# Query projection with channels on the partitions, its norm put in with the logits, in the second layer of a hybrid decoder

## The chip, the cores and the metric

The kernel is one program on one core of one Trainium2 chip. The metric is device microseconds (us) of one launch. The engines are named as the profile names them: PE is TensorE (PEld its weight loads), DVE is VectorE, ACT is ScalarE, POOL is GpSimd and SP is SyncE, which issues transfers.

## The reference, cut to what matters

Two layers over 1024 tokens of width 1024. The first is a gated DeltaNet, which the change leaves alone. The second is attention in a window of 128 keys, with 32 query heads of 64 channels that share 4 key and value heads, a norm over each query head, a bias by distance and a sink:

```
q, z = jnp.split(h @ w_in, 2, axis=-1)
q = rms_norm(q.reshape(B, T, B_Q_HEADS, B_HD), q_gain) * (B_HD ** -0.5)
logits = jnp.einsum("bnqkgd,bnskd->bnkgqs", q, k_band) + bias     # then the mask
m = jnp.maximum(jnp.max(logits, axis=-1, keepdims=True), sink)
p = jnp.exp(logits - m)
probs = p / (jnp.sum(p, axis=-1, keepdims=True) + jnp.exp(sink - m))
o = jnp.einsum("bnkgqs,bnskd->bnqkgd", probs, v_band)
return (o.reshape(B, T, B_W) * jax.nn.silu(z)) @ w_out
```

The norm of a query is one number per token and head, so it may be applied to q, or to the logits before the bias is added.

## The kernel before, in words

All large products are made in three matmuls of 32-bit operands that are split in a high and a low part: high by high, high by low, low by high. The transposed input `hT` lies in SBUF in that split form, with tokens as columns.

The second layer works in 8 groups of 4 query heads (256 channels). For each group `b_q` projects the queries, `b_z` (twice) projects the gate, and `b_attend` goes through 8 blocks of 128 tokens. Each of `b_q` and `b_z` takes its weights from a queue: a transfer of 512 KB that SP issues into `wraw` (two buffers), a multiplication by the input norm's gain on POOL (two halves, L153), a cast to the high part on ACT (L155) and a subtraction for the low part on DVE (L157). Four sets of split weights are held, so a weight can be cast only when PE has finished with the one four places earlier.

PE's order is that of the program; the other engines' orders come from a scheduler. `interleave` weaves the two strands together: `b_attend` yields amounts of time, and that much projection is put in at each yield. One block of attention goes to PE in four visits with projection between them: `turn` (four transposes of the probabilities of block i, L1197), `q_turn` (two transposes of the normalised queries of block i+3, L1149), `logits` (twelve matmuls for block i+2, L1174) and `values` (up to eight matmuls for block i-1, L1218). Around these matmuls a block needs on DVE two predicated copies (L1178) and four additions of the bias with a minimum (L1182), on ACT four exponentials (L1187), on DVE a reciprocal (L1189), and on POOL the multiplication of the probabilities by it (L1191).

Before the change `gemm_tc` (L983 to L985) projects the queries with tokens on the partitions: the stationary operand is 128 tokens of `hT`, and 256 channels are streamed. A group takes 8 x 8 x 3 = 192 such matmuls. The result is copied to SBUF (L1107), squared (L1109), summed per head (L1110), and multiplied by the inverse root (L1115); then `q_turn` transposes it for the logits. The gate already uses `gemm_ct` (L180 to L184), in which the stationary operand is 128 channels of the weight and 512 tokens are streamed.

A number of small jobs (`later`) are put off by a number of ticks; a tick is one step of contraction in `gemm_ct`, and two such steps in `gemm_tc`.

Of the kernel before, what the change touches and what calls it, by code (L numbers as in the profile page):

```python
# [18 lines left out]
P = 128  # L19
# [45 lines left out]
class Kernel:  # L65
# [122 lines left out]
    def consts(self, ctx):  # L188
# [10 lines left out]
        self.identr = cp.tile([P, P], F32R, name="identr")  # L199
        nc.vector.tensor_copy(self.identr, self.ident)  # L200
# [835 lines left out]
    class Group:  # L1036


        def __init__(self, hg):
            self.hg, self.q, self.ot, self.zs, self.left = hg, [], [], [], 5  # L1040

    def layer_b(self, last):
# [7 lines left out]
        for _ in steps:  # L1050
            for _ in range(4):
                next(first)
        for _ in first:
            pass
        self.flush()
# [5 lines left out]
        raws = lambda j: bp.tile([P, 2, 512], F32, name="qr", bufs=3)  # L1061
# [30 lines left out]
    def b_q(self, X):  # L1092

        nc, bp, sb = self.nc, self.bp, self.sb
        ws = [self.take(), self.take()]
        for half in range(2):
            qr = bp.tile([P, 4, 256], F32, name="qr", bufs=3)
            ss = sb.tile([P, 4, 4], F32, name="ssqb")
            for c in range(4):
                n = half * 4 + c  # L1100
                if c % 2 == 0:
                    ps = self.mm.tile([P, 2, 256], F32, name="mm")
                yield from self.gemm_tc(ps[:, c % 2, :], ws, n)
# [34 lines left out]
    def b_attend(self, groups):  # L1138
# [3 lines left out]
        qT, Ls, pTs = {}, {}, {}  # L1142

        def q_turn(i):
# [254 lines left out]
```

## Time and profile before

| | us |
|---|---|
| median of 3 runs | 1867.74 (1866.12 to 1868.64) |
| the profiled execution, its own time | 1867.72 |
| span of its trace | 1866.0 |
| PE busy | 1809.7 (97% of the span) |
| DVE busy | 1231.2 (66%) |
| ACT busy | 730.7 (39%) |
| POOL busy | 514.0 (28%) |

The span is from the first to the last instruction; 1.7 us of the execution's time lie outside it. Matmuls overlap in time and their ends are modelled, so the busy time of PE says only that it does not stand still; what one matmul costs is read from the distance between the starts of two neighbours. In the trace the second layer's first query projection starts at about 1130 us, its attention runs from 1155 to about 1690 us, and the output projection ends the program.

### The profile page before, as it was taken

The page shows a single profiled execution, that of the slowest core. Times are in us where ns is not written, and L with a number is a line of the kernel's source. Part 1 is how long each engine was busy: PE and PEld are TensorE (multiplying, and loading weights), DVE is VectorE, ACT ScalarE, POOL GpSimd, SP SyncE. Part 2 cuts the span into 40 slices and gives each one's busy share as a digit, 9 for nine tenths or more (in the row PEclk, how much of TensorE's full clock was granted, in tenths as well). Part 3 has the DMA queues.
Part 4 walks back from the last instruction along what each step waited for, and adds up shares of the span by engine and source line. Part 5 has one row for each costly group of instructions (what it writes and reads, how often), then busy time and mean ns, then how long its engine had stood idle before and what let it go on. Part 6 is the DMA issues. An engine that isn't in the chain of part 4 may idle for free.

```text
span 1866.0 us, 31106 instructions
## 1 busy us (share of the span) xinstructions
PE 1809.7 (97%) x11778; PEld 1466.0 (79%) x11778; DVE 1231.2 (66%) x2895; ACT 730.7 (39%) x1813; POOL 514.0 (28%) x629
## 2 busy tenths in 40 slices
PE   6999999999999998999999999999999999999999
PEld 6667778787878776778788899887787787777887
DVE  6777776868586778765545365777776766763432
ACT  6446362634445364523112042444444444441100
POOL 1323232323222233221311231333333323221211
PEclk9999999999999999999999999999999999999999
DMA  4611111112011111122655331111111111225552
GB/s 151 134 49 35 57 46 46 47 35 69 23 58 35 58 34 47 45 91 92 236 170 171 122 92 46 30 46 46 63 41 52 57 34 59 68 69 201 182 169 102
DMA packets 134874, 149.55 MB, mean 80 GB/s; under 512 B 7242, under 2 KB 91716, under 8 KB 134724
## 3 DMA queue, kind: packets, MB, share of 16 engines
q1 hardware_dynamic: 124384, 130.40, 22.5%
q10 hardware_dynamic: 10340, 17.16, 2.9%
q8 instruction: 93, 1.52, 0.3%
q14 instruction: 57, 0.47, 0.1%
HBM read 116.05 MB, written 31.49 MB: 79 GB/s over the span
## 4 chain that ended last, share of the span: by engine, by line
PE 77%; DVE 10%; issue 3%; POOL 3%; ACT 1%; DMA 1%; POOLq 0%; DVEq 0%; ACTq 0%; SPq 0%
PE mm L180 9%; PE mm L182 9%; PE mm L184 9%; PE acc L933 6%; PE acc L932 6%; PE acc L931 6%; PE mm L983 4%; PE mm L984 4%; PE mm L985 4%; PE pv L1218 3%; PE lg L1174 3%; DVE acc L494 2%; PE tp L1197 1%; DVE wlo L157 1%; PE kqp L693 1%
## 5 line engine op out<-in xcount | busy, mean ns | idle before, releaser
L180 PE MATMUL mm<-hh,whi 128*128 128x512 f32 (+1 forms) x1040 | 428.0, 412 | 2.5 <-ACT hh L246 2.4
L182 PE MATMUL mm<-hl,whi 128*128 128x512 f32 (+1 forms) x1040 | 417.9, 402 | 1.5 <-DVE hl L247 1.5
L184 PE MATMUL mm<-hh,wlo 128*128 128x512 f32 (+1 forms) x1040 | 415.4, 399 | 0.0
L157 DVE TENSOR_TENSOR wlo<-wraw,whi 128x512 fp32r<-128x512 f32 x292 | 205.8, 728 | 225.0 <-POOL whi L150 192.4
L150 POOL TENSOR_SCALAR whi<-wraw 128x1024 fp32r<-128x1024 f32 x110 | 121.3, 1103 | 474.7 <-PE acc L933 240.7
L180 PEld LDWEIGHTS mm<-hh,whi 128*128 128x128 f32 x1040 | 197.0, 189 | 39.1 <-issue 4.6
L184 PEld LDWEIGHTS mm<-hh,wlo 128*128 128x128 f32 x1040 | 196.9, 189 | 37.3 <-issue 4.2
L182 PEld LDWEIGHTS mm<-hl,whi 128*128 128x128 f32 x1040 | 197.2, 190 | 35.6 <-issue 4.2
L983 PE MATMUL mm<-whi,hh 128*128 128x256 f32 x608 | 183.6, 302 | 0.0
L984 PE MATMUL mm<-wlo,hh 128*128 128x256 f32 x608 | 171.9, 283 | 0.0
L985 PE MATMUL mm<-whi,hl 128*128 128x256 f32 x608 | 171.8, 283 | 0.0
L494 DVE SCALAR_TENSOR_TENSOR acc<-u,cw,acc 128x512 f32<-128x512 f32 x192 | 152.9, 798 | 22.0 <-POOL acc L491 19.6
L1187 ACT ACTIVATE lsb<-lsb,m 128x129 f32<-128x129 f32 x256 | 100.4, 394 | 165.2 <-DVE m L1182 129.3
L983 PEld LDWEIGHTS mm<-whi,hh 128*128 128x128 f32 x608 | 115.8, 190 | 14.7 <-issue 10.0
L1191 POOL TENSOR_TENSOR lsb<-lsb,den 128x512 f32<-128x512 f32 x64 | 72.9, 1139 | 189.2 <-DVE den L1189 177.6
L153 POOL TENSOR_TENSOR wraw<-wraw,gcolb 128x512 f32<-128x512 f32 x72 | 79.0, 1117 | 140.4 <-DMA wraw<-in_b_w_in 96.7
L984 PEld LDWEIGHTS mm<-wlo,hh 128*128 128x128 f32 x608 | 116.1, 191 | 0.2
L985 PEld LDWEIGHTS mm<-whi,hl 128*128 128x128 f32 x608 | 115.8, 190 | 0.0
L491 POOL TENSOR_SCALAR acc<-u,cw 128x512 f32<-128x512 f32 x64 | 57.0, 891 | 183.4 <-ACT u L487 169.9
L931 PE MATMUL acc<-whi,hh 128*128 128x512 f32 x256 | 99.7, 389 | 0.0
L933 PE MATMUL acc<-whi,hl 128*128 128x512 f32 x256 | 99.6, 389 | 0.0
L932 PE MATMUL acc<-wlo,hh 128*128 128x512 f32 x256 | 99.6, 389 | 0.0
(352 smaller groups left out, 3722.0 us busy)
## 6 DMA issues: line engine op xcount, KB each, us to landing
wraw<-in_a_w_in SPq DMA_DIRECT2D x48, 512.0 KB, 4.0
wraw<-in_a_w_out SPq DMA_DIRECT2D x32, 512.0 KB, 3.6
wraw<-in_b_w_in SPq DMA_DIRECT2D x32, 512.0 KB, 4.0
wraw<-in_b_w_out SPq DMA_DIRECT2D x32, 512.0 KB, 3.9
og<-zs SPq DMA_DIRECT2D x32, 256.0 KB, 2.0
ogT<-zs SPq DMA_DIRECT2D x24, 256.0 KB, 2.1
btab<-lt SPq DMA_DIRECT2D x1, 4096.0 KB, 24.3
dm<-gd SPq DMA_DIRECT2D x8, 512.0 KB, 4.1
```

What stands on the lines that cost most here:

```text
L150: nc.gpsimd.tensor_scalar(out=hi, in0=raw, scalar1=1.0, scalar2=1.0, op0=ALU.mult, op1=ALU.mult)
L157: nc.vector.tensor_tensor(out=lo[:, ks], in0=raw[:, ks], in1=self.f32(hi[:, ks]), op=ALU.subtract)
L180: nc.tensor.matmul(ps, hi[:, k, :], hh[:, k, :], start=(k == 0), stop=False)
L182: nc.tensor.matmul(ps, hi[:, k, :], hl[:, k, :], start=False, stop=False)
L184: nc.tensor.matmul(ps, lo[:, k, :], hh[:, k, :], start=False, stop=(k == KT - 1))
L494: nc.vector.scalar_tensor_tensor(out=acc, in0=u[:, t:t + 512], scalar=cw[:, t, blk:blk + 1], in1=acc, op0=ALU.mult, op1=ALU.add)
L931: nc.tensor.matmul(ps[c], oh[:, k, ts], hi[:, kk, :], start=(k4 + k == 0), stop=False)
L932: nc.tensor.matmul(ps[c], oh[:, k, ts], lo[:, kk, :], start=False, stop=False)
L933: nc.tensor.matmul(ps[c], ol[:, k, ts], hi[:, kk, :], start=False, stop=(k4 + k == 6))
L983: nc.tensor.matmul(ps, hh[:, k, ts], hi[:, k % 4, :], start=(k == 0), stop=False)
L984: nc.tensor.matmul(ps, hh[:, k, ts], lo[:, k % 4, :], start=False, stop=False)
L985: nc.tensor.matmul(ps, hl[:, k, ts], hi[:, k % 4, :], start=False, stop=(k == KT - 1))
```

## The change

The queries are now projected by `gemm_ct`: a group takes 2 halves x 2 pairs of heads x 24 = 96 matmuls with 512 columns, and the result already has the channels on the partitions, as the logits want it. It is split in high and low (`qr`, `ql`) at once, without the norm. `q_turn` is gone. The squares are transposed in 32 x 32 pieces and summed on DVE (`part`), and 16 ticks later `b_sums` adds up the pieces with one matmul against a constant and makes the inverse root of the mean square, and the root itself, in small steps on DVE. The norm goes in at the logits: a new step `rows` on POOL divides the bias by it ahead of time, and the DVE instruction that adds the bias takes the norm as its scale. `values` is emitted directly behind `logits`. The queries' weights come in the form that the gate's have. The order of projections changes by one place: the third query projection now comes ahead of the first gate projection. An unused tile is dropped.

```diff
     def b_order():
-        order = [("q", 0, 0), ("q", 1, 0), z.pop(0)]
+        order = [("q", 0, 0), ("q", 1, 0)]
         for hg in range(2, 8):
             order += [("q", hg, 0), z.pop(0), z.pop(0)]
...
     def b_q(self, X):
         ws = [self.take(), self.take()]
         for half in range(2):
-            qr = bp.tile([P, 4, 256], F32, name="qr", bufs=3)
-            ss = sb.tile([P, 4, 4], F32, name="ssqb")
-            for c in range(4):
-                n = half * 4 + c
-                if c % 2 == 0:
-                    ps = self.mm.tile([P, 2, 256], F32, name="mm")
-                yield from self.gemm_tc(ps[:, c % 2, :], ws, n)
-                if c % 2 == 0:
-                    continue
-                two = qr[:, c - 1:c + 1, :]
-                nc.vector.tensor_copy(two, ps)
...
-            rq = self.rsqrt(sb, ss, [P, 4, 4], "rqb")
-            qv = qr.rearrange("p n (h d) -> p n h d", h=4)
-            nc.vector.tensor_tensor(out=qv, in0=qv, in1=rq.unsqueeze(3).broadcast_to([P, 4, 4, 64]), op=ALU.mult)
-            X.q.append(qv)
+            part = sb.tile([P, 2, 16], F32, name="part")
+            for pr in range(2):
+                ps = self.mm.tile([P, 512], F32, name="mm")
+                yield from self.gemm_ct(ps, ws[pr], half)
+                if pr == 0:
+                    hi = bp.tile([P, 2, 512], F32R, name="qr", bufs=4)
+                    lo = bp.tile([P, 2, 512], F32R, name="ql", bufs=4)
+                nc.scalar.copy(out=hi[:, pr, :], in_=ps)
+                sq = sb.tile([P, 8, 64], F32, name="sq", bufs=1).rearrange("p n d -> p (n d)")
+                nc.scalar.activation(out=sq, in_=ps, func=AF.Square)
+                nc.vector.tensor_tensor(out=lo[:, pr, :], in0=ps, in1=self.f32(hi[:, pr, :]), op=ALU.subtract)
...
+                sqT = sb.tile([P, 512], F32, name="sqT", bufs=1)
+                nc.vector.transpose(out=sqT, in_=sq)
+                nc.vector.tensor_reduce(out=part[:, pr, :], in_=sqT.rearrange("p (b c) -> p b c", c=32), op=ALU.add,
...
+            X.q.append((hi, lo))
+            self.later(16, lambda part=part: self.b_sums(X, part))
+
+    def b_sums(self, X, part):
...
+        nc.vector.tensor_scalar(out=two[:, :, 0, :], in0=part, scalar1=first, scalar2=None, op0=ALU.mult)
+        nc.vector.tensor_tensor(out=two[:, :, 1, :], in0=part, in1=two[:, :, 0, :], op=ALU.subtract)
+        ps = self.aps.tile([P, 512], F32, name="tp", bufs=3)[:, 0:64]
+        nc.tensor.matmul(ps, self.same, two.rearrange("p r a b -> p (r a b)"), start=True, stop=True)
...
+        rq = self.rsqrt(sb, ss, [P, 4, 4], "rqb")
+        nc.vector.scalar_tensor_tensor(out=ss, in0=ss, scalar=-2.0, in1=rq, op0=ALU.mult, op1=ALU.mult)
+        X.norm.append((rq, ss))
...
+        def rows(i):
...
+            L = Ls[i] = bp.tile([P, 4, P + 1], F32, name="lsb", bufs=3)
+            nc.gpsimd.tensor_copy(L[:, :, P:P + 1], self.sink[:, 4 * X.hg:4 * X.hg + 4].unsqueeze(2))
+            rms = X.norm[n // 4][1][:, :, n % 4:n % 4 + 1]
+            nc.gpsimd.tensor_tensor(out=L[:, :, 0:P], in0=X.bias, in1=rms.broadcast_to([P, 4, P]), op=ALU.mult)
...
-                    nc.vector.tensor_tensor_reduce(out=L[:, e, 0:P], in0=ps[:, pr, P:256], in1=X.bias[:, e, :],
-                                                   scale=1.0, scalar=sk[:, e:e + 1], op0=ALU.add, op1=ALU.min,
-                                                   accum_out=m[:, e:e + 1])
+                    nc.vector.tensor_tensor_reduce(out=L[:, e, 0:P], in0=ps[:, pr, P:256], in1=L[:, e, 0:P],
+                                                   scale=scale[:, e, n % 4:n % 4 + 1], scalar=sk[:, e:e + 1],
+                                                   op0=ALU.add, op1=ALU.min, accum_out=m[:, e:e + 1])
...
-        fill = (1.2, 1.2, 0.6, 0.6, 1.2)
         for i, (X, n) in enumerate(blocks):
             turn(i)
-            yield fill[0]
-            if i + 3 <= last:
-                q_turn(i + 3)
-            yield fill[1]
+            yield 2.4
+
             if i + 2 <= last:
                 logits(i + 2)
-            yield fill[2]
+            if i:
+                values(i - 1)
+            if i + 3 <= last:
+                rows(i + 3)
+            yield 1.2
...
-            yield fill[3]
-            if i:
-                values(i - 1)
-            yield fill[4]
+            yield 1.2
```

The first place where instructions stand differently is PE's order in the middle of the attention. `lg` is the logits' product, `pv` the values', `mm` a projection's, `tp` a transpose's or the sums'. Before:

```order
L1174 MATMUL lg<-kh,qTl 128x256 x2
L1174 MATMUL lg<-kl,qT 128x256 x2
L983 MATMUL mm<-whi,hh_87 128x256
L984 MATMUL mm<-wlo,hh_87 128x256
L985 MATMUL mm<-whi,hl_88 128x256
L983 MATMUL mm<-whi,hh_87 128x256
L984 MATMUL mm<-wlo,hh_87 128x256
L985 MATMUL mm<-whi,hl_88 128x256
L1218 MATMUL pv<-pT_12430,vv 64x256 x2
L1218 MATMUL pv<-pT_12427,vv 64x256 x2
L983 MATMUL mm<-whi,hh_87 128x256
```

After, in a stretch that also has one of the 16 matmuls of `b_sums` (L1122):

```order
L1184 MATMUL lg<-kh,qr 128x256 x2
L1184 MATMUL lg<-kh,ql 128x256 x2
L1184 MATMUL lg<-kl,qr 128x256 x2
L1228 MATMUL pv<-pT_12233,vv 64x256 x2
L1228 MATMUL pv<-pT_12230,vv 64x256 x2
L182 MATMUL mm<-hl_86,whi 128x512
L184 MATMUL mm<-hh_85,wlo 128x512
L1122 MATMUL tp<-two,cst 128x64
L180 MATMUL mm<-hh_83,whi 128x512
L182 MATMUL mm<-hl_84,whi 128x512
```

The values' matmuls have moved up against the logits', and no projection stands between the two.

The second place is POOL's order at the start of the attention, where the weights' multiplications by the gain (L153) for the first eight weights of the layer stand in a row. Before:

```order
L1046 MEMSET neg 128x1
L1165 COPY lsb<-sink 128x4 x3
L153 TENSOR_TENSOR wraw<-wraw,gcolb 128x512 x16
L1191 TENSOR_TENSOR lsb<-lsb,den 128x4x128 x2
L1165 COPY lsb<-sink 128x4
L1191 TENSOR_TENSOR lsb<-lsb,den 128x4x128
```

After:

```order
L1044 MEMSET neg 128x1
L1163 COPY lsb<-sink 128x4 x3
L153 TENSOR_TENSOR wraw<-wraw,gcolb 128x512 x16
L1165 TENSOR_TENSOR lsb<-bias,ssqb 128x4x128 x3
L1201 TENSOR_TENSOR lsb<-lsb,den 128x4x128 x2
L1163 COPY lsb<-sink 128x4
```

The multiplication of the bias for the first three blocks (L1165 of the changed kernel) stands behind the sixteenth of the weights' multiplications; before, the first POOL instruction of the attention at that place was the multiplication of the finished probabilities (L1191).

## Rows read from the trace of the kernel before

**Rows 1.** Busy time by engine in two stretches: engines' us (instructions), PE clock, DMA.

```profile
1155.00:1170.00 15.00, 11.65 (x81) 10.57 (x79) 13.04 (x45) 7.40 (x22) 7.10 (x6) 0.77 0.24 71
1170.00:1690.00 520.00, 520.00 (x3701) 415.25 (x3700) 371.23 (x1196) 241.64 (x776) 171.76 (x229) 1.00 0.18 55
```

**Rows 2.** Waits of POOL, 1170 to 1690 us: total us, times, longest.

```profile
POOL lsb L1191 <- DVE den L1189: 176.5, 45, 7.9
POOL wraw L153 <- DMA wraw<-in_b_w_in: 70.3, 18, 7.4
```

**Rows 3.** Timeline of PE, two unbroken runs of projection: start us, modelled duration.

```profile
1099.77 0.28 PE L985 MATMUL mm<-whi,hl 128*128 128x256 f32 x1
...
1102.89 0.28 PE L984 MATMUL mm<-wlo,hh 128*128 128x256 f32 x1
...
1666.22 0.39 PE L184 MATMUL mm<-hh,wlo 128*128 128x512 f32 x1
...
1667.85 0.40 PE L180 MATMUL mm<-hh,whi 128*128 128x512 f32 x1
```

**Rows 4.** Timeline of PE around one visit of the queries' transposes.

```profile
1301.16 0.38 PE L1149 MATMUL tp<-cst,qr 128*128 128x128 f32 x2
1301.30 0.36 PE L983 MATMUL mm<-whi,hh 128*128 128x256 f32 x1
1301.50 0.28 PE L984 MATMUL mm<-wlo,hh 128*128 128x256 f32 x1
```

**Rows 5.** Timeline of PE around one visit of the logits.

```profile
1660.45 0.39 PE L182 MATMUL mm<-hl,whi 128*128 128x512 f32 x1
1660.77 0.39 PE L1174 MATMUL lg<-kh,qT 64*128 64x256 f32 x2
...
1661.47 0.28 PE L1174 MATMUL lg<-kl,qT 64*128 64x256 f32 x2
1661.68 0.51 PE L184 MATMUL mm<-hh,wlo 128*128 128x512 f32 x1
1662.02 0.39 PE L180 MATMUL mm<-hh,whi 128*128 128x512 f32 x1
```

**Rows 6.** Timeline of PE around the first layer's like sums, two matmuls.

```profile
64.98 0.29 PE L552 MATMUL tr<-part,cst 128*128 128x16 f32 x2
65.12 0.48 PE L180 MATMUL mm<-hh,whi 128*128 128x512 f32 x1
65.44 0.40 PE L182 MATMUL mm<-hl,whi 128*128 128x512 f32 x1
```

**Rows 7.** PE at the attention's start: two waits (timeline), and a stretch's clock.

```profile
1161.23 0.35 PE L1174 MATMUL lg<-kh,qT 64*128 64x256 f32 x1 [1.66 <-DVE m L1182]
1163.17 0.58 PE L1174 MATMUL lg<-kh,qT 64*128 64x256 f32 x1 [1.59 <-DVE m L1182]
1164.00:1169.00 5.00, 5.00 (x29) 4.78 (x28) 4.20 (x14) 2.03 (x9) 3.92 (x4) 0.50 0.00 0
```

**Rows 8.** Timelines of ACT, DVE and POOL at the attention's start.

```profile
1155.09 1.05 ACT L155 CAST whi<-wraw 128x1024 fp32r<-128x1024 f32 x1 [0.39 <-PE mm L985]
1158.25 0.69 DVE L157 TENSOR_TENSOR wlo<-wraw,whi 128x512 fp32r<-128x512 f32 x1
1163.75 3.02 POOL L153 TENSOR_TENSOR wraw<-wraw,gcolb 128x512 f32<-128x512 f32 x2 [0.93 <-ACT lsb L1187]
```

**Rows 9.** Groups by line: busy us, mean ns of one, idle before.

```profile
L1191 POOL TENSOR_TENSOR lsb<-lsb,den 128x512 f32<-128x512 f32 x64 | 72.9, 1139 | 189.2 <-DVE den L1189 177.6
L1182 DVE CUSTOM_DVE_ANT_0 lsb<-lg,bias,sink 128x128 f32<-128x128 f32 x256 | 76.4, 343 | 0.0
L546 DVE STREAM_TRANSPOSE sqT<-acc 128x512 f32<-128x512 f32 x16 | 11.2, 703 | 0.9 <-ACT acc L541 0.8
```

**Rows 10.** Timeline of DVE, one small instruction without and with POOL at work.

```profile
1159.82 0.16 DVE L118 TENSOR_TENSOR rqbt<-rqbt,rqby 128x16 f32<-128x16 f32 x1
1161.00 0.84 DVE L118 TENSOR_TENSOR rqbt<-rqbt,rqby 128x16 f32<-128x16 f32 x1
...
1160.78 2.03 POOL L153 TENSOR_TENSOR wraw<-wraw,gcolb 128x512 f32<-128x512 f32 x2 [20.06 <-DVE m L1182]
```

More of the change, by code (lines that the diff above doesn't have):

```diff
@@ L1039, in __init__ @@
         def __init__(self, hg):
-            self.hg, self.q, self.ot, self.zs, self.left = hg, [], [], [], 5
+            self.hg, self.q, self.norm, self.ot, self.zs, self.left = hg, [], [], [], [], 5
     def layer_b(self, last):
@@ L1050, in layer_b @@
         for _ in steps:
-            for _ in range(4):
+            for _ in range(12):
                 next(first)
@@ L1059, in layer_b @@
             back.append(self.b_q(X[hg]) if kind == "q" else self.b_z(X[hg], j))
-        raws = lambda j: bp.tile([P, 2, 512], F32, name="qr", bufs=3)
+        raws = lambda j: self.f32(bp.tile([P, 2, 512], F32R, name="qr", bufs=4))
         def ahead():
@@ new lines, in b_q @@
+            X.q.append((hi, lo))
+            self.later(16, lambda part=part: self.b_sums(X, part))
+    def b_sums(self, X, part):
+        nc, sb = self.nc, self.sb
+        two = sb.tile([P, 2, 2, 16], F32, name="two")
+        first = self.cst[:, C_TRI + 63:C_TRI + 64]
+        nc.vector.tensor_scalar(out=two[:, :, 0, :], in0=part, scalar1=first, scalar2=None, op0=ALU.mult)
+        nc.vector.tensor_tensor(out=two[:, :, 1, :], in0=part, in1=two[:, :, 0, :], op=ALU.subtract)
+        ps = self.aps.tile([P, 512], F32, name="tp", bufs=3)[:, 0:64]
+        nc.tensor.matmul(ps, self.same, two.rearrange("p r a b -> p (r a b)"), start=True, stop=True)
+        two = two.rearrange("p r a b -> p (r a) b")
+        nc.vector.tensor_tensor(out=two, in0=ps.rearrange("p (e b) -> p e b", e=4), op=ALU.mult,
+                                in1=self.group.unsqueeze(1).broadcast_to([P, 4, 16]))
+        ss = sb.tile([P, 4, 4], F32, name="ssqb")
+        nc.vector.tensor_reduce(out=ss, in_=two.rearrange("p e (n g) -> p e n g", g=4), op=ALU.add, axis=AX.X)
+        nc.vector.tensor_scalar(out=ss, in0=ss, scalar1=1.0 / 64, scalar2=EPS, op0=ALU.mult, op1=ALU.add)
+        rq = self.rsqrt(sb, ss, [P, 4, 4], "rqb")
+        nc.vector.scalar_tensor_tensor(out=ss, in0=ss, scalar=-2.0, in1=rq, op0=ALU.mult, op1=ALU.mult)
+        X.norm.append((rq, ss))
@@ L1141, in b_attend @@
         blocks = [(X, n) for X in groups for n in range(NB)]
[L1142 to L1144 removed]
+        Ls, pTs = {}, {}
+        def rows(i):
             X, n = blocks[i]
[L1146 to L1154 removed]
+            L = Ls[i] = bp.tile([P, 4, P + 1], F32, name="lsb", bufs=3)
+            nc.gpsimd.tensor_copy(L[:, :, P:P + 1], self.sink[:, 4 * X.hg:4 * X.hg + 4].unsqueeze(2))
+            rms = X.norm[n // 4][1][:, :, n % 4:n % 4 + 1]
+            nc.gpsimd.tensor_tensor(out=L[:, :, 0:P], in0=X.bias, in1=rms.broadcast_to([P, 4, P]), op=ALU.mult)
         def logits(i):
@@ L1160, in logits @@
             sk = self.sink[:, 4 * X.hg:4 * X.hg + 4]
-            qh, ql = qT.pop(i)
+            qh, ql = (t[:, :, n % 4 * P:n % 4 * P + P] for t in X.q[n // 4])
+            L, scale = Ls[i], X.norm[n // 4][0]
             k0 = 0 if n else P
             ksl = slice((n - 1) * P + k0, (n + 1) * P)
-            L = Ls[i] = bp.tile([P, 4, P + 1], F32, name="lsb", bufs=3)
-            nc.gpsimd.tensor_copy(L[:, :, P:P + 1], sk.unsqueeze(2))
             m = sb.tile([P, 4], F32, name="m")
@@ L1224, in b_attend @@
         last = len(blocks) - 1
-        q_turn(0)
+        rows(0)
+        rows(1)
         yield 1.0
         logits(0)
-        q_turn(1)
+        rows(2)
         yield 1.5
         logits(1)
-        q_turn(2)
         yield 2.5
-        fill = (1.2, 1.2, 0.6, 0.6, 1.2)
         steps = iter(())
@@ L1367, in weights @@
                 for k in range(2):
-                    yield four(bin_, k, hg, gain(2 + k))
+                    yield col(bin_, 2 * hg + k, self.gcolb[:, 8:16])
             else:
```

18 lines of the change are left out of this document (1 added, 17 removed).

## The prediction

> **What bounds the kernel now.** I read the busy times first, cut into stretches. From 1170 to 1690 us, the second layer's attention with its projections, PE is busy for 520.00 of 520 us, DVE for 371.23, ACT for 241.64, POOL for 171.76 [rows 1]; the clock is at its full level. Next the waits: in this stretch the list for PE is empty, while POOL is often idle before it multiplies the probabilities [rows 2]. So here time is the sum of PE's steps from one matmul's start to the next's, and what the change is worth is read from the distances of starts. The exception is the 15 us at the start of the attention, where PE is busy for 11.65 only and the mean clock is 0.77 [rows 1]: there PE waits for the first blocks' work on DVE [rows 7]. The rest of the program (the first layer, the output projection) isn't touched.
>
> **The change, part by part.**
>
> *Queries' matmuls.* In an unbroken run of 256-column matmuls 26 steps take 1102.89 - 1099.77 = 3.12 us, 0.120 each; of 512-column ones 7 steps take 1.63 us, 0.233 each [rows 3]. A group now has 96 of 0.233 (22.37 us) in place of 192 of 0.120 (23.04 us): -0.67 us, and for 8 groups -5.4 us. The starts are rounded to 0.01 us and other short runs give 0.119, so this is -4 to -6. [...]
>
> *Queries' transposes.* The visit goes from 1301.16 to the second projection matmul behind it at 1301.50, 0.34 us, where one ordinary step of 0.12 would have stood [rows 4]: 0.22 us. It holds two short transposes and a first matmul that is 0.08 late (0.20 instead of 0.12). 64 visits go: -14.1 us. The ACT cast and the DVE subtraction behind them go as well.
>
> *Values behind the logits.* The step into the logits takes 1660.77 - 1660.45 = 0.32 us, 0.09 over an ordinary 0.23; the step off their last pair 0.21; and the first projection matmul behind them 0.34, 0.11 over [rows 5]. With the values directly behind, one entry (0.09) and one late first matmul (0.11) are saved, if the step off the last pair stays at 0.21 whatever follows. That is 0.20 x 63 = 12.6 us. The trace has no step from logits to values. If that step cost 0.32 us like an entry from a projection, 0.11 of the saving would go: 5.7 us. I take the upper end, since the step off a pair is a row of just these matmuls, and keep both for the range.
>
> *Sums.* Sixteen matmuls of 128 x 64 are new. In the first layer two like them, with 16 columns, take 0.14 us, and the first matmul behind them 0.32, 0.09 over [rows 6]. One with four times the columns I take at 0.14 + 0.09 + 0.01 = 0.24 us: +3.8 us (bounds 0.20 and 0.35 us each: +3.2 to +5.6). Since they come 16 ticks, some 11 us, behind the last matmul of their half, and the squares' transposing and summing takes 2 to 3 us on DVE, PE shouldn't wait for them.
>
> *DVE, ACT and POOL.* DVE gets 32 subtractions, 32 transposes and 32 sums at about 0.70 us each [rows 9], 67 us, and loses 32 copies and sums, 16 multiplications and 64 subtractions of similar size; even with nothing lost, its 149 idle us of 520 would hold them. ACT exchanges copies and squares. The bias's addition now reads its scale from SBUF; the first layer's instructions of that kind and size take 0.34 us as this one does [rows 9], so I price it at nothing. POOL gets 64 multiplications like L1191's, 1.14 us each [rows 9]: 73 us on top of 171.76, 47% of the stretch. They are hidden by POOL's idle time before the probabilities' multiplication, 176.5 us in 45 waits, 3.9 us on average [rows 2]. The weights' transfers keep their size, and their form is one that the gate's have already; they stay hidden.
>
> *The start.* Here the change adds to what is waited for. Call T0 the end of the first group's last matmul; before, it is at about 1155.07, where ACT can cast the sixth weight [rows 8]. That weight's buffer is free when DVE has subtracted, 1158.25 + 0.69 = 1158.94; then the eighth weight is loaded into it, and POOL's multiplications of that weight begin at 1163.75, 4.81 us later, and take 3.02 [rows 8]. In the changed order the bias of the first three blocks stands behind them on POOL, and the first block's additions (L1182) wait for it; behind these wait the second block's logits on PE, for their PSUM. I reckon: cast until T0 + 1.1; the subtractions, with a few small steps between, until T0 + 2.9; load until T0 + 7.7; two multiplications, 2.03 to 3.02 us [rows 8, 10], until T0 + 10; the first block's bias, 1.04 to 1.14, T0 + 11.1; four additions at 0.35, T0 + 12.5. PE has until then the sum, five projection matmuls, the first logits and seven more: 4.4 us. So it waits 8.1 us. Before it waited 1.66 + 1.59 = 3.25 [rows 7]: +4.8 us. Before, the clock then stood at 0.50 for 5 us [rows 7], which costs 2.5; I take the same after.
>
> *The sum.* -5.4 - 14.1 - 12.6 + 3.8 + 4.8 = -23.5 us. POOL's queue is fuller, and some blocks will be late where a weight's transfer holds it (up to 7.4 us [rows 2]); for this I add 1.5 us. That gives -22, and from the profiled execution's 1867.72 us (span 1866.0 and 1.7 around it, and 0.02 from the median of the runs) 1846 us.
>
> **The rivals.**
>
> A. *The saving at the values is small and the start dearer.* The step from logits to values costs 0.32, and the clock stays low for twice as long at the start (+2.5): -23.5 + 6.9 + 2.5 = -14, 1854 us. For it: the two weights' shapes of the values are another kind than the projection's. Against it: the step off the logits is one number, 0.21, whatever follows.
>
> B. *The start costs nothing more.* Since the first weight of a pair is now free half a projection earlier, the seventh and eighth weights could land sooner than I reckon, so that PE waits as before: -28 us, 1840. Against it: the sixth weight's cast still needs the very last matmul.
>
> C. *POOL becomes the wait.* Place: the probabilities' multiplication of a block, now behind the next block's bias on POOL. If it comes 1.14 us later in each block and nothing hides that, 64 x 1.14 = 73 us: 1867.7 - 28.3 + 73 = 1912 us, slower. It decides from 28.3 / 64 = 0.44 us a block. Against it: in 45 of 64 blocks POOL stood idle before this multiplication. For it: in the other blocks it was behind other work, 18 times a transfer [rows 2]; if just these 18 blocks lose 1.14 and as much again by the queue behind, 41 us would be too much already, and with 1.14 to 1.5 in them 21 to 27 us, no change.
>
> D. *DVE is held up by POOL.* A small DVE instruction with two operands in SBUF takes 0.16 us, and 0.84 while POOL multiplies [rows 10]. Each of the 16 halves has nine such steps in a chain: if all nine fall under POOL's work, 9 x 0.68 = 6.1 us later. For the first half this would add to the start as far as the chain overtakes the eighth weight: T0 + 4 + 6.1 is still not behind T0 + 10, so it adds little; in later halves it would make DVE busy for 98 us more, 469 of 500, and then some blocks would be late: 16 x 0.4 = 6 us, 1852. [...]
>
> E. *The change doesn't do what it says*: with 512 columns the visits' costs grow, or a scheduler's order undoes the gain. The order shows the visits merged; a visit behind 512 columns costs the same as one behind 256 [rows 4, 5]. I see no ground for it but the size of the rebuilding.
>
> **How the numbers follow.** My forecast (1841 to 1851) 0.57, A 0.14, B 0.10, D 0.06, C 0.09 (two thirds of it slower, a third no change), E 0.04 (half slower, half no change). A measurement here can tell 0.2%, 3.7 us, from no change. Faster is 0.57 + 0.14 + 0.10 + 0.06 = 0.87; no change 0.05; slower 0.08. The range goes from B's end to behind A: 1837 to 1859 us; it leaves out C and E, and the far ends of the others, 2 in 10 together.
>
> **What would show it.** No transposes of queries and no step of 0.20 behind them; steps of 0.233 us in the query projections; a step from logits to values of 0.21 us (0.32 in A); one gap of about 8 us on PE behind the first logits, with the bias's multiplication on POOL behind the eighth weight's, and a stretch at the half clock behind it; no further PE wait; POOL busy near 47%, DVE near 72% of the stretch. The prediction is wrong if PE's waits name the probabilities or POOL in the middle of the attention, if the steps at a visit grow, or if the sums' matmul waits for DVE.

## The result, and the profile after

The changed kernel takes 1853.35 us (median of 6 runs, 1851.83 to 1861.42) against 1868.24 for the kernel before in the same session (6 runs): a ratio of 0.9925, with a 95% interval from 0.9908 to 0.9942. It is 14.9 us faster; I had forecast 22. The profiled execution takes 1851.83 us, its span is 1850.1.

Both traces have a first part that the change doesn't touch, so I measured the second layer apart: from the last copy of its values (`vv`) to the first matmul of the output projection. That is 1131.15 to 1687.79 before and 1130.23 to 1671.95 after, 556.6 and 541.7 us: -14.9. The other 1.0 us of the spans' difference (1866.0 less 1850.1) lies in parts that the change doesn't touch.

The first view is again the busy times by stretch, in the columns of [rows 1]:

```profile
1150.00:1175.00 25.00, 16.80 (x78) 12.79 (x77) 15.54 (x52) 7.81 (x22) 10.85 (x11) 0.80 0.15 43
1175.00:1675.00 500.00, 495.22 (x2949) 370.89 (x2949) 398.36 (x1233) 233.93 (x741) 233.74 (x288) 1.00 0.19 57
```

PE no longer works without a break: 495 of 500 us. POOL is at 47%, as reckoned; DVE is at 80%, where I had reckoned 72%. The waits say what PE waits for (1100 to 1700 us: total us, times, longest), and below them, as in [rows 2], what POOL waits for:

```profile
PE lg L1184 <- DVE m L1192: 11.7, 5, 8.1
PE tp L1207 <- POOL lsb L1201: 0.6, 1, 0.6
PE lg L1184 <- DVE two L1119: 0.3, 1, 0.3
```

```profile
POOL lsb L1201 <- DVE den L1199: 111.5, 31, 7.1
POOL wraw L153 <- DMA wraw<-in_b_w_in: 60.9, 14, 7.9
```

One wait of 8.1 us is the start. The others, 4.7 us together, stand in the middle (at 1206, 1313, 1418, 1514 us and smaller ones), where there was none. POOL still has long idle times before the probabilities, so it isn't POOL's queue that is full. DVE waits for POOL too (1175 to 1675 us), at the step that writes a new norm (`ssqb`):

```profile
DVE ssqb L1127 <- POOL lsb L1165: 12.2, 7, 3.6
```

That tile has two buffers in the kernel, so the step has to wait until POOL has made the last bias with the norm of two halves before. The kernel before has no such wait.

PE's timeline at one visit, against [rows 3, 5]:

```profile
1385.45 0.40 PE L184 MATMUL mm<-hh,wlo 128*128 128x512 f32 x1
1385.78 0.39 PE L1184 MATMUL lg<-kh,qr 64*128 64x256 f32 x2
...
1386.47 0.28 PE L1184 MATMUL lg<-kl,qr 64*128 64x256 f32 x2
1386.69 1.08 PE L1228 MATMUL pv<-pT,vv 128*64 128x256 f32 x8
1387.70 0.50 PE L180 MATMUL mm<-hh,whi 128*128 128x512 f32 x1
1388.04 0.39 PE L182 MATMUL mm<-hl,whi 128*128 128x512 f32 x1
1388.27 0.39 PE L184 MATMUL mm<-hh,wlo 128*128 128x512 f32 x1
```

The step from the logits to the values takes 1386.69 - 1386.47 = 0.22 us here and 0.207 on the mean of 61; it is the 0.21 with which the logits end before (0.208 on the mean of 64); the 0.32 of an entry occurs once, behind the wait at 1418. One entry (0.33) and one late first matmul (0.34) are left of two each. The sums, against [rows 6], take 0.14 and make the next matmul 0.08 late:

```profile
1152.77 0.33 PE L1122 MATMUL tp<-two,cst 128*128 128x64 f32 x2
1152.91 0.48 PE L180 MATMUL mm<-hh,whi 128*128 128x512 f32 x1
1153.22 0.39 PE L182 MATMUL mm<-hl,whi 128*128 128x512 f32 x1
```

The start, timelines of DVE, POOL and PE, against [rows 7, 8]. T0, the end of the first group's last matmul, is at 1152.77 now:

```profile
1155.55 1.53 DVE L157 TENSOR_TENSOR wlo<-wraw,whi 128x512 fp32r<-128x512 f32 x1
...
1160.93 0.17 DVE L1130 SCALAR_TENSOR_TENSOR ssqb<-ssqb,rqby 128x16 f32<-128x16 f32 x1
1164.27 0.41 DVE L1192 CUSTOM_DVE_ANT_0 lsb<-lg,lsb,sink 128x128 f32<-128x128 f32 x1 [3.17 <-POOL lsb L1165]
```

```profile
1161.19 2.04 POOL L153 TENSOR_TENSOR wraw<-wraw,gcolb 128x512 f32<-128x512 f32 x2 [4.65 <-DVE ssqb L1130]
1163.18 3.06 POOL L1165 TENSOR_TENSOR lsb<-bias,ssqb 128x512 f32<-128x512 f32 x3
```

```profile
1165.07 1.24 PE L1184 MATMUL lg<-kh,qr 64*128 64x256 f32 x2 [8.12 <-DVE m L1192]
```

The bias stands on POOL behind the eighth weight, as I had said, and the wait is 8.12 us, as I had said. But the norm that the bias needs is ready only at 1161.10, T0 + 8.3, where I had T0 + 4.

Last, groups by line in 1175 to 1675 us (busy us, mean ns of one), after, and one of before that was not shown:

```profile
L1192 DVE CUSTOM_DVE_ANT_0 lsb<-lg,lsb,sink 128x128 f32<-128x128 f32 x248 | 88.2, 404 | 0.1
L157 DVE TENSOR_TENSOR wlo<-wraw,whi 128x512 fp32r<-128x512 f32 x56 | 47.0, 851 | 5.8 <-ACT whi L155 4.7 <-POOL whi L150 0.5 <-PE lg L1184 0.3
L1165 POOL TENSOR_TENSOR lsb<-bias,ssqb 128x512 f32<-128x512 f32 x60 | 66.5, 1109 | 5.4 <-DVE den L1199 5.4
```

```profile
L157 DVE TENSOR_TENSOR wlo<-wraw,whi 128x512 fp32r<-128x512 f32 x56 | 38.8, 698 | 12.4 <-ACT whi L155 12.3
```

The bias's addition, 343 ns in [rows 9], takes 404. The subtraction for a weight's low part, an instruction that the change does not touch, has gone from 698 to 851.

### The profile page after: what moved, and what is told of

Its sections match the earlier page's. It is cut to its first block, busy times and chain, and to the rows that moved or that the text cites. A ratio compares the mean times of both kernels' runs of the same rounds, so it can differ in the third digit from the quotient of the medians.

```text
span 1850.1 us, 29358 instructions
## 1 busy us (share of the span) xinstructions
PE 1784.9 (96%) x10914; PEld 1414.9 (76%) x10914; DVE 1257.7 (68%) x2926; ACT 724.0 (39%) x1781; POOL 585.0 (32%) x693
## 4 chain that ended last, share of the span: by engine, by line
PE 71%; DVE 14%; issue 4%; POOL 3%; ACT 2%; DMA 1%; POOLq 0%; ACTq 0%; DVEq 0%; SPq 0%
PE mm L180 11%; PE mm L182 11%; PE mm L184 11%; PE acc L931 6%; PE acc L930 6%; PE acc L929 6%; PE pv L1228 3%; DVE acc L492 3%; PE lg L1184 2%; DVE wlo L157 2%; PE kqp L691 1%; PE sc L798 1%; PE tp L1207 1%; PE kqp L666 1%; PE sc L807 1%
## 5 line engine op out<-in xcount | busy, mean ns | idle before, releaser
L180 PE MATMUL mm<-hh,whi 128*128 128x512 f32 (+1 forms) x1296 | 530.6, 409 | 2.7 <-ACT hh L244 2.6
L182 PE MATMUL mm<-hl,whi 128*128 128x512 f32 (+1 forms) x1296 | 518.7, 400 | 1.7 <-DVE hl L245 1.5
L184 PE MATMUL mm<-hh,wlo 128*128 128x512 f32 (+1 forms) x1296 | 516.6, 399 | 0.0
L180 PEld LDWEIGHTS mm<-hh,whi 128*128 128x128 f32 x1296 | 246.0, 190 | 52.7 <-issue 9.9
L182 PEld LDWEIGHTS mm<-hl,whi 128*128 128x128 f32 x1296 | 246.1, 190 | 49.0 <-issue 8.0
L153 POOL TENSOR_TENSOR wraw<-wraw,gcolb 128x512 f32<-128x512 f32 x72 | 81.8, 1155 | 149.1 <-DMA wraw<-in_b_w_in 79.6
L1192 DVE CUSTOM_DVE_ANT_0 lsb<-lg,lsb,sink 128x128 f32<-128x128 f32 x256 | 91.1, 404 | 3.2 <-POOL lsb L1165 3.2
L929 PE MATMUL acc<-whi,oh 128*128 128x512 f32 x192 | 76.0, 396 | 0.0
L931 PE MATMUL acc<-whi,ol 128*128 128x512 f32 x192 | 75.9, 395 | 0.0
L930 PE MATMUL acc<-wlo,oh 128*128 128x512 f32 x192 | 75.5, 393 | 0.0
L1165 POOL TENSOR_TENSOR lsb<-bias,ssqb 128x512 f32<-128x512 f32 x64 | 70.6, 1105 | 5.4 <-DVE den L1199 5.4
```

The lines of the kernel that those rows point to most:

```text
L153: nc.gpsimd.tensor_tensor(out=raw[:, ks], in0=raw[:, ks], op=ALU.mult, in1=gain[:, ks].unsqueeze(2).broadcast_to([P, shape[0] // 2, shape[ ...
L180: nc.tensor.matmul(ps, hi[:, k, :], hh[:, k, :], start=(k == 0), stop=False)
L182: nc.tensor.matmul(ps, hi[:, k, :], hl[:, k, :], start=False, stop=False)
L184: nc.tensor.matmul(ps, lo[:, k, :], hh[:, k, :], start=False, stop=(k == KT - 1))
L929: nc.tensor.matmul(ps[c], oh[:, k, ts], hi[:, kk, :], start=(k4 + k == 0), stop=False)
L930: nc.tensor.matmul(ps[c], oh[:, k, ts], lo[:, kk, :], start=False, stop=False)
```

## The theories and the runs

Theory: PE's own steps save what was forecast, and what is missing is given back in waits. They come from DVE, whose instructions with two operands in SBUF take longer while POOL works (rival D, which I had priced at 6 us and given 0.06; the subtraction goes from 698 to 851 ns, while `pT<-tp,cst`, of the same size with an operand in PSUM, stays at 688 and 682), with the dearer addition making it worse. One wait in the middle shows it, DVE and then POOL:

```profile
1410.84 1.01 DVE L119 SCALAR_TENSOR_TENSOR rqby<-rqbt,rqby 128x16 f32<-128x16 f32 x1
1411.77 0.68 DVE L1215 TENSOR_TENSOR pT<-tp,cst 128x512 f32<-128x512 f32 x1
1412.37 0.47 DVE L117 TENSOR_TENSOR rqbt<-ssqb,rqby 128x16 f32<-128x16 f32 x1
1412.88 0.17 DVE L118 TENSOR_TENSOR rqbt<-rqbt,rqby 128x16 f32<-128x16 f32 x1
1413.09 0.91 DVE L119 SCALAR_TENSOR_TENSOR rqby<-rqbt,rqby 128x16 f32<-128x16 f32 x1
1414.04 0.55 DVE L1130 SCALAR_TENSOR_TENSOR ssqb<-ssqb,rqby 128x16 f32<-128x16 f32 x1
```

```profile
1410.78 1.04 POOL L153 TENSOR_TENSOR wraw<-wraw,gcolb 128x512 f32<-128x512 f32 x1 [4.17 <-DMA wraw<-in_b_w_in]
1411.78 1.04 POOL L1201 TENSOR_TENSOR lsb<-lsb,den 128x512 f32<-128x512 f32 x1
1412.76 0.19 POOL L1163 COPY lsb<-sink 128x4 f32<-128x4 f32 x1
1412.90 1.06 POOL L1165 TENSOR_TENSOR lsb<-bias,ssqb 128x512 f32<-128x512 f32 x1
1413.93 0.63 POOL L1212 TENSOR_SCALAR_AFFINE_SELECT pT<-pT 128x512 f32<-128x512 f32 x1
```

Small steps of 0.17 us take 1.01, 0.47, 0.91 and 0.55, and each ends where a POOL instruction ends (1411.85 and 1411.82, 1412.84 and 1412.82, 1414.00 and 1413.96, 1414.59 and 1414.56). That is 2.26 us lost in DVE's order, and behind it stand the next block's additions, for which PE waits 0.98 and 0.28 us at 1418. Rivals: POOL's queue itself is the wait (C); DVE simply has too much to do; DVE is stopped by its waits for the norm's buffer; the saving on PE is smaller than reckoned.

All runs, with the second layer's stretch as above and PE's waits of over 0.15 us in it (the sum of the gaps; before 556.6 and 3.25, after 541.7 and 12.85). The ratio is to the kernel before in the same session. The whole change also drops a flush of the put-off jobs behind the first query projection and sets the size of a scratch area for transfers; no run tests these two apart.

| run | median us | ratio, 95% interval | stretch | PE waits |
|---|---|---|---|---|
| e1_start_dve | 1852.10 | 0.9918 (0.9904 to 0.9932) | 540.8 | 13.03 |
| e1_early_sums | 1848.43 | 0.9899 (0.9885 to 0.9912) | 534.0 | 6.23 |
| e2_merge_only | 1856.11 | 0.9933 (0.9919 to 0.9946) | 543.0 | 3.19 |
| e4_cols256 | 1854.42 | 0.9934 (0.9921 to 0.9946) | 542.6 | 9.88 |
| e5_scale_const | 1848.05 | 0.9890 (0.9878 to 0.9903) | 537.5 | 11.02 |
| e6_pool_twice | 1876.79 | 1.0050 (1.0036 to 1.0063) | 566.8 | 28.73 |
| e7_rows_dve | 1845.79 | 0.9877 (0.9864 to 0.9890) | 532.8 | 7.98 |
| e8_newton_pool | 1877.65 | 1.0051 (1.0036 to 1.0066) | 563.6 | 25.32 |
| e9_both | 1842.58 | 0.9855 (0.9838 to 0.9872) | 528.9 | 4.13 |
| e10_both_act | 1840.21 | 0.9843 (0.9827 to 0.9860) | 527.8 | 3.56 |
| e11_pool_memset | 1859.20 | 0.9949 (0.9930 to 0.9968) | 546.3 | 15.18 |
| e12_transposes | 1863.51 | 0.9969 (0.9957 to 0.9981) | 550.4 | 9.90 |

**The start: POOL's queue, or the norm?** First the bias of three blocks on DVE:

```diff
-            nc.gpsimd.tensor_tensor(out=L[:, :, 0:P], in0=X.bias, in1=rms.broadcast_to([P, 4, P]), op=ALU.mult)
+            (nc.vector if i < 3 else nc.gpsimd).tensor_tensor(out=L[:, :, 0:P], in0=X.bias, in1=rms.broadcast_to([P, 4, P]), op=ALU.mult)
```

> The first three blocks' bias is multiplied on DVE, all later ones stay on POOL. The prediction's step: the 8.12 us for which PE waits at the start are the eighth weight's multiplications on POOL, behind which the bias stands. If that is all, the bias is ready at about T0 + 5.5 in place of T0 + 11.4 and the wait falls to about 2.5 us: 1847 us. The rival, from the trace after: the norm itself is ready only at 1161.10, T0 + 8.3, since its small steps on DVE lie between the sixth weight's subtractions and under POOL's multiplications. Then the bias on DVE (0.7 to 1.5 us a block, under POOL's next multiplications from 1161.2) gives the wait 6 to 8 us: 0 to 2 us gained, 1851 to 1853 us.

The wait is 7.05 us, 1.1 less. The rival holds: with the bias off POOL's queue, the late norm and the bias behind it on DVE still hold PE for 7.05 of the 8.1 us. Second, the first half's sums early:

```diff
-            self.later(16, lambda part=part: self.b_sums(X, part))
+            self.later(16 if X.hg or half else 4, lambda part=part: self.b_sums(X, part))
```

> Only the very first half's sums come 4 ticks behind their matmuls in place of 16; so the norm is ready before the sixth weight's cast, and the scheduler puts the first three bias rows ahead of the seventh and eighth weights on POOL. If the start's wait is made of late norm and POOL's queue, as the trace after says, what is left is DVE's work until about 1158.6 and two additions: the wait falls from 8.1 us to 2 to 3, and with a shorter stretch at the half clock the time is 1846 to 1848 us. The rival: something else holds the first block (a transfer of the bias, ACT's table load, the second block's logits by another buffer); then the wait stays over 6 us and the time is 1851 to 1853 us.

The wait is 1.85 us, and a new one of 1.03 stands before the sums' matmul, which now comes too soon for its own sums: 4.9 us faster by the medians and 7.8 by the stretch. So the start's wait comes of the late norm and of POOL's order, and the early norm takes away both: on POOL the bias now stands ahead of the eighth weight and begins at 1153.55 (timelines of DVE and POOL). What an early norm behind the old order on POOL would give, no run shows.

```profile
1153.29 0.18 DVE L1130 SCALAR_TENSOR_TENSOR ssqb<-ssqb,rqby 128x16 f32<-128x16 f32 x1
1153.91 2.70 DVE L157 TENSOR_TENSOR wlo<-wraw,whi 128x512 fp32r<-128x512 f32 x2 [0.44 <-ACT whi L155]
```

```profile
1153.55 3.97 POOL L1165 TENSOR_TENSOR lsb<-bias,ssqb 128x512 f32<-128x512 f32 x3 [8.80 <-DVE ssqb L1130]
```

**The terms on PE.** The merged visit alone, on the kernel before:

```diff
+            if i:
+                values(i - 1)
             yield fill[2]
...
-            yield fill[3]
-            if i:
-                values(i - 1)
-            yield fill[4]
+            yield fill[3]
```

> The kernel before with one part of the change alone: the values' matmuls directly behind the logits', the two fills around them put together, everything else (256-column queries, their transposes) as before. The prediction's term: -12.6 us, 1855.5 us. What the trace after showed (12.3 us at the visits' edges, but 1.7 more within the logits): -10.5, 1857.5 us. The rival, its lower bound (the step from logits to values costs as much as an entry): -5.7 us, 1862.5 us.

11.2 us faster by the medians, 13.7 by the stretch. In the trace the visits' edges lose 12.1 us (60 of 63 entries to the values 5.5, late first matmuls 6.4, one step 0.2) and the steps within the logits stay as they were, 44.12 against 44.11 us; most of the rest of the 13.7 is a shorter stretch at the half clock (18 steps there in place of 30), which need not come from the edit (see the last section). So the term of 12.6 is right within 0.5 us, and what the logits' steps grew by in the changed kernel (45.85 us) belongs to its waits.

The queries in 256 columns, within the changed kernel:

```diff
-                yield from self.gemm_ct(ps, ws[pr], half)
+                yield from self.gemm_256(ps, ws[pr], half)
...
+        for s in range(2):
+            ts = slice(256 * s, 256 * s + 256)
...
+                nc.tensor.matmul(ps[:, ts], hi[:, k, :], hh[:, k, :], start=(k == 0), stop=False)
+                yield 0.1075
...
```

> The changed kernel, with the queries' 768 matmuls of 512 columns cut into 1536 of 256 columns (channels still on the partitions, each with its own weight load, ticks and fills kept). The prediction's term backwards: 768 x (0.240 - 0.233) = +5.4 us, 1858.7 us. [...]

Only 1.1 us slower. But the steps cost what I had reckoned: an unbroken run (first and last of 17 starts)

```profile
1269.75 0.28 PE L184 MATMUL mm<-hl,whi 128*128 128x256 f32 x1
...
1271.67 0.28 PE L186 MATMUL mm<-hh,wlo 128*128 128x256 f32 x1
```

has 1.92 / 16 = 0.120 us a step, and the mean of all 512-column steps of the changed kernel is 0.231 (351.2 us for 1520): 768 x (0.240 - 0.231) = 6.9 us more. Three us of it only fill waits (12.85 to 9.88 us), and the clock falls no more in the middle (it is at 1.00 in each 50 us from 1200 to 1650; in the changed kernel it is granted 0.57 of its full level from 1420 to 1424 us, behind the waits at 1418).

The transposes put back:

```diff
-            yield 2.4
+            yield 1.2
+            if i + 3 <= last:
+                ...
+                for pr in range(2):
+                    nc.tensor.transpose(out=ps[:, pr, :], in_=qv[:, pr, b % 4 * P:b % 4 * P + P], identity=self.ident)
+            yield 1.2
```

> The changed kernel with the 61 visits of two query transposes put back on PE between the projection's matmuls, into a PSUM tile that nobody reads (no cast and no subtraction behind them). The prediction's term backwards: 61 x 0.22 = +13.4 us, 1866.8 us. The rival: since PE now also waits for DVE at the start and in the middle, part of these 13 us only fills waits (up to the 4.7 us in the middle and what they cost in clock, 1.7): +7 us, 1860 us.

10.2 us slower, between the two. In the trace the 61 visits cost 6.63 + 1.67 + 5.09 = 13.4 us, 0.22 each, as reckoned; the waits shrink by 2.95 us (in the middle from 4.7 to 1.6). The stretch is 8.7 us longer, 1.75 less than these two give; the half clock in the middle of the changed kernel (0.50 from 1420.3 to 1423.7 us) costs 1.7 by an estimate, half of its 3.4 us. Both are the rival's reason.

**Where the waits come from.** The scale as a constant:

```diff
-                                                   scale=scale[:, e, n % 4:n % 4 + 1], scalar=sk[:, e:e + 1],
+                                                   scale=1.0, scalar=sk[:, e:e + 1],
```

> The changed kernel, but the bias's addition takes the constant 1.0 as its scale in place of the pointer to the norm (the norm of the logits is left out). The addition writes in place as in the changed kernel. If the pointer is what made one of these 404 ns long in place of 343, it is back near 343 and DVE has 15 us less to do in 64 blocks. If DVE's load as such makes the 4.7 us of PE waits in the middle of the attention, most of these go: 2 to 4 us faster than the changed kernel, 1850 us. The rival: in place or not is what costs, 404 stays, and the waits with it: 1853 us. The start's wait of 8 us (bias and norm late) stays in both, since the bias is still multiplied.

The group of the additions in 1175 to 1675 us:

```profile
L1192 DVE CUSTOM_DVE_ANT_0 lsb<-lg,lsb,sink 128x128 f32<-128x128 f32 x248 | 75.1, 344 | 0.1
```

344 ns (the run leaves the norm out of the logits): the pointer costs the 60 ns, not the writing in place. The waits in the middle fall to 2.76 us (11.02 less the start's 8.26), the time by 5.3 us. (DVE's order is another one here too, so the 5.3 us are not the 60 ns alone.) POOL's multiplication twice:

```diff
             nc.gpsimd.tensor_tensor(out=L[:, :, 0:P], in0=X.bias, in1=rms.broadcast_to([P, 4, P]), op=ALU.mult)
+            nc.gpsimd.tensor_tensor(out=L[:, :, 0:P], in0=X.bias, in1=rms.broadcast_to([P, 4, P]), op=ALU.mult)
```

> The changed kernel with each block's bias multiplication on POOL done twice (64 more of 1.05 to 1.14 us: POOL busy for 60% of the stretch in place of 47%). If POOL's new work is hidden, as the prediction priced it: within 4 us of the changed kernel beside 1 to 2 us at the start, 1853 to 1857 us. The rival (POOL's queue becomes the wait, C): 64 x 1 us, up to 1917 us. A third, that POOL's work holds up DVE's instructions with two operands in SBUF (D): the waits in the middle named by DVE grow from 4.7 to 10 or 15 us, 1858 to 1864 us.

23.4 us slower than the changed kernel. It is the third theory in kind. Without the start's wait (8.1 us, here 10.3), the waits named by DVE's additions grow from 3.6 to 12.2 us, as it expected; those named by POOL are 2.3 us, and the subtraction is at 960 ns. The time grows by more than it expected: of 25.1 us by the stretch PE's waits are 15.9, and more steps at the half clock (92) cost about 7. The rows are of the waits and of the groups by line:

```profile
PE lg L1185 <- DVE m L1193: 22.5, 12, 10.3
PE tp L1208 <- POOL lsb L1202: 2.3, 3, 1.2
```

```profile
L157 DVE TENSOR_TENSOR wlo<-wraw,whi 128x512 fp32r<-128x512 f32 x56 | 53.2, 960 | 8.0 <-ACT whi L155 4.6 <-POOL whi L150 3.3
```

As much POOL time, by instructions that read nothing from SBUF:

```diff
+            nc.gpsimd.memset(L[:, :, 0:P], 0.0)
+            nc.gpsimd.memset(L[:, :, 0:P], 0.0)
             nc.gpsimd.tensor_tensor(out=L[:, :, 0:P], in0=X.bias, in1=rms.broadcast_to([P, 4, P]), op=ALU.mult)
```

> The changed kernel with two more POOL instructions per block that only write (the block's bias rows are filled with zero twice, 2 x 0.5 us, ahead of the multiplication), as much POOL time as the doubled multiplication, which cost 23 us. If what costs is that POOL's instructions with two operands in SBUF hold DVE's back: DVE's subtractions for the weights stay at 0.85 us, the waits at about 5 us in the middle, and the time is 1853 to 1857 us. If it is the time on POOL's queue as such: 1870 us or more.

Its windows row and the subtraction's group:

```profile
1175.00:1675.00 500.00, 492.95 (x2916) 368.21 (x2916) 397.25 (x1227) 231.60 (x739) 291.28 (x408) 0.99 0.19 56
```

```profile
L157 DVE TENSOR_TENSOR wlo<-wraw,whi 128x512 fp32r<-128x512 f32 x56 | 47.1, 852 | 5.9 <-ACT whi L155 4.7 <-POOL whi L150 1.1
```

POOL is busy for 291 us, nearly as with the doubled multiplication (298.61), but the subtraction stays at 852 ns, and the time is 5.9 us over the changed kernel, not 23.4: 2 us above what I expected of the first theory and far from the second. In both runs DVE also stands longer at the norm's step (12.2 us in the changed kernel; the doubled multiplication first):

```profile
DVE ssqb L1127 <- POOL lsb L1166: 16.7, 6, 4.0
DVE ssqb L1127 <- POOL lsb L1167: 15.2, 7, 4.1
```

This is a second way from POOL to PE, and the traces tell how much it carries. After such a wait of over 1 us DVE works without a pause, in the changed kernel for 0.9 to 6.2 us (five times). The waits of PE that end in such a time are 0.2 of the 4.7 us in the middle in the changed kernel, 2.9 of 7.1 with the memsets and 4.4 of 18.4 with the doubled multiplication. So it explains what the memsets add, but of what the doubled multiplication adds 9.5 us lie outside it. The two runs keep POOL busy for as long; they differ in what the added instructions read, and in their length (0.53 us each with the memsets, 1.1 with the multiplication). No run varies the length alone, but the memsets don't lengthen the subtraction at all (852 ns against 851; 960 with the multiplication). So by these two runs it is mostly what POOL's instructions read, not how long POOL works; in what way the one holds up the other, they don't show.

Then all bias multiplications on DVE, the busier engine (the first diff, without `if i < 3`):

> The changed kernel with all 64 bias multiplications on DVE in place of POOL: POOL's share as in the kernel before (34%), DVE's 64 x 0.7 us = 45 us more, from 79% to 88%. If DVE's load makes the waits in the middle, these grow from 4.7 us to well over 10: 1860 us or more. If POOL's instructions beside DVE's are the cause, they shrink to under 3 although DVE has more to do: 1850 us.

PE's waits, 1100 to 1700 us, and the windows row:

```profile
PE lg L1184 <- DVE m L1192: 8.0, 3, 7.0
```

```profile
1175.00:1675.00 500.00, 499.00 (x2981) 374.83 (x2980) 425.34 (x1299) 235.08 (x742) 188.41 (x229) 1.00 0.20 61
```

7.6 us faster, with DVE at 85%: 0.9 us of waits is left in the middle. DVE's load as such is not the cause. The subtraction is shorter again:

```profile
L157 DVE TENSOR_TENSOR wlo<-wraw,whi 128x512 fp32r<-128x512 f32 x58 | 43.0, 758 | 3.0 <-ACT whi L155 1.5 <-POOL whi L150 1.4
```

The run takes away both ways from POOL to PE: DVE's list of waits has none for the norm's buffer here. By the count above that one is worth little in the changed kernel, but no run takes it away alone. One attempt to relieve DVE went the other way, the Newton steps of the inverse root on POOL, on top of the early sums:

```diff
+            if pool_steps:
+                nc.gpsimd.tensor_tensor(out=t, in0=x, in1=y, op=ALU.mult)
+                nc.gpsimd.tensor_tensor(out=t, in0=t, in1=y, op=ALU.mult)
+                nc.gpsimd.tensor_scalar(out=t, in0=t, scalar1=1.5, scalar2=None, op0=ALU.add)
+                nc.gpsimd.tensor_tensor(out=y, in0=t, in1=y, op=ALU.mult)
```

> The early sums at the start, and the three Newton steps of the inverse root in the sums taken from DVE to POOL (twelve small POOL instructions for nine on DVE, 16 times). If the waits in the middle come from the chain of small steps in DVE's order, each held up by POOL and holding up the logits behind it, 2 to 4 us of the 4.7 go: 1845 us beside 1848.4 with the early sums alone. The rival: POOL's queue gets the chain's delays in its turn, and the probabilities wait behind it: 1848 us or more.

```profile
L1136 DVE SCALAR_TENSOR_TENSOR ssqb<-ssqb,rqby 128x16 f32<-128x16 f32 x15 | 5.1, 339 | 62.4 <-POOL rqby L121 62.4
```

29.2 us slower than the early sums alone; the row is of the groups by line, with the idle time before it last. The rival has the sign right but names the wrong engine: DVE itself stands 62.4 us (15 times, up to 7.4) before the step that takes POOL's result, and the additions stand behind that step. Last, what helped put together, and in the second run the probabilities' multiplication on ACT too:

> Early sums for the very first half and all bias multiplications on DVE together. The start's wait, 8.1 us in the changed kernel, 2.1 with early sums, now has two or three bias multiplications of 0.7 us on DVE ahead of the first additions: 3 to 4 us. The middle keeps the under 1 us of waits that it has with the bias on DVE. 1845.8 - 3 to 4 and 1 for the shorter half clock: 1841 to 1843 us. The rival: DVE is now the bound at the start and takes it all back, 1845 to 1847 us.

> As the one above, and the multiplication of the probabilities taken from POOL to ACT as well (four instructions with a pointer scale for one): POOL busy for 23% of the stretch in place of 38%, ACT for 60% in place of 47%. If what POOL's work does to DVE still costs PE something, 1 to 2 us faster than the one above; since only 0.9 us of waits were left in the middle, 0 to 1 us is the most that I see. The rival: ACT's queue gets longer, its casts of weights and probabilities come later, and PE waits for these: 2 us slower or more.

```diff
-            nc.gpsimd.tensor_tensor(out=p, in0=p, in1=den.unsqueeze(2).broadcast_to([P, 4, P]), op=ALU.mult)
+            for e in range(4):
+                nc.scalar.activation(out=p[:, e, :], in_=p[:, e, :], func=AF.Copy, scale=den[:, e:e + 1])
```

The windows row of the second:

```profile
1175.00:1675.00 500.00, 499.56 (x2978) 375.75 (x2977) 404.82 (x1287) 305.96 (x984) 115.19 (x168) 1.00 0.21 66
```

1842.58 us, as expected, and 1840.21: 13.1 us faster than the changed kernel and 1.6% than the one before. The last step gains 2.4 us by the medians but 1.0 by the stretch, so how much of it is real stays open.

## Why the prediction was right, and where it was off

The direction, the range and the steps on PE were right; the total was 7 us too good, outside the 1841 to 1851 us to which I had given 0.57. Of the signs, "no further PE wait" and DVE near 72% failed, and one wait of 0.6 us in the middle names the probabilities. By the terms:

- **Queries' matmuls**, -5.4: the mean steps (2 x 0.1195 for 256 columns before, 0.231 for 512 after) give 768 x 0.008 = -6.1.
- **Queries' transposes**, -14.1: -13.9 (the visits' rows of before, summed), and 13.4 for the 61 put back.
- **Values behind the logits**, -12.6: -12.3 at the edges in the changed kernel, -12.1 with this part alone. I had counted 63 visits, but the last two blocks' values have no logits ahead of them: 61 x 0.20 = 12.2. Rival A's dear step occurs once in 61.
- **Sums**, +3.8: 16 x (0.055 + 0.083 + 0.085) = +3.6, from the step between the two halves, the step off them and the late first matmul, if each sum has all three. The sums' matmul waits nowhere.
- **Start**, +4.8: 8.12 - 3.25 = +4.9. The size is right, the way to it only in part. The eighth weight's multiplications and the bias come at T0 + 8.4 and T0 + 10.4 (predicted 7.7 and 10), but the norm was late too, T0 + 8.3 in place of T0 + 4, as DVE's small steps lay between two subtractions for weights (one of 1.53 us, under POOL) and then, with POOL idle, between the second half's subtraction, transposing and summing. That the first half's sums came after a full half of other work was the price; 4 ticks take most of it away.
- **Scattered waits**, +1.5: this is the step that failed. There are 4.7 us of waits in the middle, 1.7 us more in the steps within the logits (45.85 against 44.11 us, most of it in the five steps with a wait, which are longer by more than the gap), and 1.8 us more for steps at the half clock, behind the start and behind the wait at 1418 (half of 9.44 us in 29 steps less half of 5.88 in 30). Together 8.2 us, 6.7 more than allowed.

With these the sum is -6.1 - 13.9 - 12.3 + 3.6 + 4.9 + 8.2 = -15.6; measured are -14.9 in the stretch, and 0.7 us stays unassigned.

The step behind it is "DVE, ACT and POOL": the new POOL work was called hidden by POOL's idle time before the probabilities. That cover was the wrong one to look at. POOL is never what PE waits for but once (0.6 us); its work lengthens DVE's instructions (698 to 851 ns for one that nobody changed), and DVE's order has the next block's additions behind them. The taking of the addition's scale from SBUF, priced at nothing, costs 61 ns x 256 = 15.6 us of DVE. Rival D had DVE's instructions longer under POOL, and it put the later halves at 6 us. That this is near the 8.2 is partly luck: it let the nine small steps of a half take 6.1 us more and DVE work 469 of 500 us. Measured, they take 2.9 us in all (2.6 before, from the means of L117 to L119) and DVE works 398; larger instructions grew (the subtraction, the addition), and two of PE's waits are followed by steps at a lower clock (0.50 from 1166 to 1171 us behind the start's, 0.57 from 1420 to 1424 behind the one at 1418; behind those at 1206, 1313 and 1514 it is 1.00), which D left out. No term or rival had DVE's 12.2 us of waits for the norm's buffer; by the count above they reach PE with 0.2 us here. And PE's savings and DVE's waits are not independent: the less PE has to do between two visits, the sooner DVE is late. The two runs that give PE work back (e4, e12) get 3 us of waits back for it, so the last 3 us that PE saved bought nothing.

## What to carry to other kernels

An engine with idle time is free room only for its own queue; ask what its instructions do to those of another engine at the same moment, and find that in the trace as the same instruction being longer (here 698 to 851 ns), not only as a wait. When the bound engine gets faster, as PE by 29 us here (6.1 + 13.9 + 12.3 - 3.6), the slack of the next engine shrinks by as much, so price its longest chain at the new pace. Work that needs two operands in SBUF may be better on the busier DVE than on the idle POOL beside it: here it was, by 7.6 us, though the move also took away DVE's waits for the norm's buffer. A small tile that one engine writes and another reads much later can stop the writer (DVE for 12.2 us in 7 waits here): count its buffers by its last reader.

## What the hardware showed that I had not expected

- The DVE instruction of the bias takes 404 ns with a pointer to its scale and 344 with a constant, 128 x 128 elements in both.
- Two POOL instructions a block that only write (0.53 us each) cost 5.9 us where one of the same length (1.1 us) that reads two operands costs 23.4.
- PE at a lower clock outside the change: behind the same wait of 2.1 us in the first layer, the clock is full (1.00) in the changed kernel's profile and at 0.73 in another one with the same instructions there (e9), windows in the columns of [rows 1]:

```profile
660.00:666.00 6.00, 6.00 (x31) 4.73 (x31) 4.13 (x11) 4.79 (x11) 1.29 (x2) 1.00 0.56 169
```

```profile
662.00:668.00 6.00, 6.00 (x25) 5.14 (x26) 4.08 (x8) 3.98 (x9) 1.09 (x1) 0.73 0.29 97
```

Such stretches come in different number in different executions: outside the second layer's stretch they add up to 4.9 us in the profile of e11 and to 18.8 in that of e9, and the time outside it is 1307.7 and 1313.7 us, 6.0 apart with no cause in the edit. Why, the runs don't tell. For parts worth under 5 us the stretch in question is the better measure than the total.
